# Block products of a triangular inverse issued in interleaved pairs, and the final norm's statistics taken for several row tiles at once

## The chip, the cores and the metric

The kernel runs on one core of one Trainium2 chip. The metric is the device time of one execution in microseconds; the time of a kernel is the median of three runs.

## The reference

One inference step of a one-layer decoder: 512 prompt rows and 8 sample rows of width 1024 go through a first norm, one combined input projection, two mixers side by side (sparse attention and a gated DeltaNet), an output projection, a squared-ReLU MLP and a final norm. Two places matter here.

In the DeltaNet, prompt rows are cut into chunks; for each chunk and head a unit lower triangular matrix is inverted:

```python
lmat = jnp.where(strict, jnp.einsum('...id,...jd->...ij', kb, k) * decay, 0.0)
tmat = lax.linalg.triangular_solve(eye + lmat, jnp.broadcast_to(eye, lmat.shape),
                                   left_side=True, lower=True, unit_diagonal=True)
```

At the very end every row is normed:

```python
y = xf * lax.rsqrt(jnp.mean(xf * xf, axis=-1, keepdims=True) + EPS)
return (y * g.astype(jnp.float32)).astype(x.dtype)
```

## The kernel before, in words

The kernel works on 4 chunks of 128 rows and 8 heads, so 32 matrices of 128x128, held in the tile LU (called M in this part, `M[row, m, column]`, m from 0 to 31).

**The weight stream.** All big products are units of one list (`units`): a unit takes a 128-column slice of a weight matrix (a load of 512 KB on SP's queue into one of 4 buffers, line 352), splits it in two parts on ACT and DVE (lines 398 to 402), and multiplies in 24 products per half of the rows (lines 450 to 453). Units called "a" (ada, line 257) make modulation vectors: two loads of 512 KB, then `quarters` (line 163), which issues products of 32 weight columns for four column groups of the array in turn, all 128 rows high, and two small products after it. Units may have a gate that opens only when other work was issued.

**Order.** `run` (line 475) merges generators with this stream: a `yield x` says that x * 1.6 us of stream products (by the program's own count, `pe_time`) may go ahead of the generator's next step. What the generators issue has a higher priority than the stream (line 484). The final order on each engine is set at build time by a list scheduler with a simulated timeline.

**The inverse** is in `triangular` (lines 1012 to 1122). The 32x32 blocks on the diagonal (called A, B, C, D, at partitions 0, 32, 64, 96) are inverted element by element on DVE; then off-diagonal blocks follow from products of 32x32 blocks (lines 1089 to 1105) and of 64x64 blocks (lines 1107 to 1122). `blocks` (line 1080) takes one PSUM bank, issues one product per matrix into it, 16 or 8 of one kind in a row, and returns it; DVE or ACT then take the bank out (lines 1092, 1093, 1100, 1101, 1104, 1110, 1119, 1121). Each of these fp32 products shows as two weight loads and two matmuls in the trace. Four kinds follow one another:

- first, 64 products of 32x32: rows B of the array into columns A, and rows D into columns C (lines 1090, 1091);
- second, 96 of 32x32: rows A into columns A, rows C into columns C, rows A into columns B (lines 1098, 1099, 1103);
- third, 32 of 64x64: upper half of the rows (64 to 127) into the lower half of the columns (line 1109);
- fourth, 32 of 64x64: lower half of the rows into the lower half of the columns (line 1115).

Banks with the tags "sc" and "pt" are four in all (line 142), given out in turn. After `triangular`, `recurrence` (line 1129) uses LU; the stream units left at that point are ada units, and then units whose gate `recurrence` opens. TA, iv and St are tiles of a pool of 5 buffers (`q4`).

**The end** is `final` (line 1920), called for row tiles 0 and 1, and then for 2, 3 and 4 (4 holds the sample rows). As the last projection's columns come in, a tile's 128x128 pieces are transposed on PE; after 4 pieces ACT squares and sums 512 columns (line 1936). Then, tile by tile: DVE adds two sums, `rstd` (line 273) scales on DVE and takes the power -1/2 on GpSimd (line 277), DVE and ACT scale the two halves (lines 1946, 1947), and SP stores both (line 1949).

## Time and profile before

| | us |
|---|---|
| three runs | 1317.97, 1320.69, 1319.63 (median 1319.63) |
| profiled execution | 1317.83 |
| its span, first to last instruction | 1315.8 |
| mean granted clock of TensorE in the span | 0.967 of full speed |
| PE busy in the span | 1230.0 (93%) |
| DVE, ACT, GpSimd busy | 845.6, 647.7, 237.9 |

A time in the trace counts from the first instruction of the span. PE is the matmul part of TensorE, PEld its weight loads, POOL is GpSimd, SP and ACT with a q are queues that issue transfers. An arrow "<-" before a name gives what ended an engine's idle time. A group's mean is the time of one instruction from start to end; matmuls overlap in the pipeline, so the distance of two starts, not the mean, is what one costs.

### The profile page before, as it was taken

The page shows a single profiled execution, that of the slowest core. Times are in us where ns is not written, and L with a number is a line of the kernel's source. Part 1 is how long each engine was busy: PE and PEld are TensorE (multiplying, and loading weights), DVE is VectorE, ACT ScalarE, POOL GpSimd, SP SyncE. Part 2 cuts the span into 40 slices and gives each one's busy share as a digit, 9 for nine tenths or more (in the row PEclk, how much of TensorE's full clock was granted, in tenths as well). Part 3 has the DMA queues.
Part 4 walks back from the last instruction along what each step waited for, and adds up shares of the span by engine and source line. Part 5 has one row for each costly group of instructions (what it writes and reads, how often), then busy time and mean ns, then how long its engine had stood idle before and what let it go on. Part 6 is the DMA issues. An engine that isn't in the chain of part 4 may idle for free.

```text
span 1315.8 us, 26700 instructions
## 1 busy us (share of the span) xinstructions
PE 1230.0 (93%) x10356; PEld 1161.2 (88%) x10356; DVE 845.6 (64%) x2294; ACT 647.7 (49%) x1552; POOL 237.9 (18%) x326
## 2 busy tenths in 40 slices
PE   4898899999989999899998899999999999999997
PEld 2698899989978989687788798989999999999997
DVE  2585868795356788886777787886843334334355
ACT  3484847754234345655555766673543133133134
POOL 2111110112121110321221332330331031030000
PEclk9899999999689999899999899999999999999999
DMA  8852412334252445335434221452723333333433
GB/s 255 231 163 75 134 36 65 99 84 130 73 148 68 129 118 153 113 108 164 136 98 153 74 71 49 128 161 66 208 65 97 89 91 95 97 91 87 133 108 114
DMA packets 235874, 149.82 MB, mean 114 GB/s; under 512 B 10330, under 2 KB 231058, under 8 KB 235484
## 3 DMA queue, kind: packets, MB, share of 16 engines
q1 hardware_dynamic: 226436, 135.84, 36.4%
q0 software_dynamic: 2240, 6.38, 1.8%
q10 hardware_dynamic: 7072, 5.90, 1.5%
q8 instruction: 81, 1.33, 0.4%
q14 instruction: 45, 0.37, 0.1%
HBM read 136.87 MB, written 15.60 MB: 116 GB/s over the span
## 4 chain that ended last, share of the span: by engine, by line
PE 45%; DVE 7%; ACT 3%; DMA 2%; issue 2%; POOL 1%; POOLq 0%; SPq 0%; ACTq 0%; DVEq 0%
PE bpg L153 36%; PE bsp L160 3%; PE bek L153 3%; PE bsp L153 2%; PE bek L169 1%; DVE wl L402 1%; DVE ptl L1490 1%; DMA raw<-in_w_in 1%; DMA raw<-in_w_up 1%; ACT ps L1458 0%; DMA raw<-in_w_out 0%; DVE wh L400 0%; ACT pw L1458 0%; DVE hl L1516 0%; DVE ps L1434 0%
## 5 line engine op out<-in xcount | busy, mean ns | idle before, releaser
L153 PE MATMUL bpg<-hh,wh 128*128 128x256 f32 (+1 forms) x1168 | 342.3, 293 | 5.9 <-ACT LU L705 1.9
L153 PE MATMUL bpg<-hh,wl 128*128 128x256 f32 (+1 forms) x1168 | 337.0, 289 | 1.8 <-DVE wl L402 1.8
L153 PE MATMUL bpg<-hl,wh 128*128 128x256 f32 (+1 forms) x1168 | 337.7, 289 | 0.0
L153 PEld LDWEIGHTS bpg<-hh,wh 128*128 128x128 f32 x1168 | 225.4, 193 | 11.6 <-ACT LU L705 2.5
L153 PEld LDWEIGHTS bpg<-hh,wl 128*128 128x128 f32 x1168 | 224.3, 192 | 4.2 <-DVE wl L402 3.1
L153 PEld LDWEIGHTS bpg<-hl,wh 128*128 128x128 f32 x1168 | 225.2, 193 | 1.8 <-issue 0.6
L402 DVE TENSOR_TENSOR wl<-raw,wh 128x1024 fp32r<-128x1024 f32 x149 | 182.4, 1225 | 66.9 <-PE bpg L153 35.8
L153 PE MATMUL bpg<-act,wh 128*128 128x264 f32 (+1 forms) x1024 | 186.7, 284 | 0.0
L398 ACT CAST wh<-raw 128x1024 fp32r<-128x1024 f32 x117 | 121.5, 1048 | 119.2 <-PE bpg L153 54.6
L153 PEld LDWEIGHTS bpg<-act,wh 128*128 128x128 f32 x1024 | 157.9, 188 | 0.1
L153 PE MATMUL bpg<-act,wl 128*128 128x264 f32 (+1 forms) x512 | 145.1, 284 | 0.2 <-DVE wl L402 0.2
L153 PE MATMUL bpg<-h2h,wl 128*128 128x256 f32 (+1 forms) x448 | 126.7, 283 | 0.3 <-DVE wl L402 0.3
L153 PE MATMUL bpg<-h2h,wh 128*128 128x256 f32 (+1 forms) x448 | 126.6, 283 | 0.0
L153 PE MATMUL bpg<-h2l,wh 128*128 128x256 f32 (+1 forms) x448 | 126.4, 282 | 0.0
L1842 POOL TENSOR_TENSOR r<-r 128x520 f32<-128x520 f32 (+2 forms) x40 | 60.1, 1502 | 285.7 <-ACT r L1841 281.4
L1805 DVE SCALAR_TENSOR_TENSOR o_dn<-bpg,consts,o_dn 128x256 f32<-128x256 f32 x80 | 38.2, 483 | 102.7 <-PE bpg L153 102.7
L153 PEld LDWEIGHTS bpg<-act,wl 128*128 128x128 f32 x512 | 96.3, 188 | 0.5 <-DVE wl L402 0.4
L1841 ACT ACTIVATE r<-bpg 128x256 f32<-128x256 f32 (+1 forms) x64 | 24.6, 386 | 137.1 <-PE bpg L153 137.1
L153 PEld LDWEIGHTS bpg<-h2h,wl 128*128 128x128 f32 x448 | 84.3, 188 | 0.5 <-DVE wl L402 0.5
L153 PEld LDWEIGHTS bpg<-h2l,wh 128*128 128x128 f32 x448 | 84.4, 188 | 0.0
L153 PEld LDWEIGHTS bpg<-h2h,wh 128*128 128x128 f32 x448 | 84.3, 188 | 0.0
L153 PE MATMUL bsp<-K,qst 128*128 128x256 f32 (+6 forms) x288 | 69.1, 319 | 5.8 <-DVE rounded L1481 2.0
(633 smaller groups left out, 2478.4 us busy)
## 6 DMA issues: line engine op xcount, KB each, us to landing
raw<-in_w_in SPq DMA_DIRECT2D x68, 512.0 KB
wa<-in_w_ada SPq DMA_DIRECT2D x48, 512.0 KB
raw<-in_w_down SPq DMA_DIRECT2D x40, 512.0 KB
raw<-in_w_up SPq DMA_DIRECT2D x36, 512.0 KB
raw<-in_w_out SPq DMA_DIRECT2D x12, 512.0 KB
Sx<-in_state_dn SPq DMA_DIRECT2D x16, 256.0 KB
out_s_dn<-Sx SPq DMA_DIRECT2D x16, 256.0 KB
pg<-in_cache_k_slc SPq DMA_DIRECT2D x16, 128.0 KB
```

The source lines that it names most:

```text
L153: nc.tensor.matmul(out, lhs, rhs, start=start, stop=stop)
L160: nc.tensor.transpose(out, in_, idn)
L169: r = nc.tensor.matmul(out[32 * j:32 * j + 32], lhs(j, s), rhs(j, s), start=start and s == 0, stop=stop and s == n - 1)
L398: nc.scalar.copy(out=wh, in_=raw)
L402: nc.vector.tensor_tensor(wl[:, 0:kp], raw[:, 0:kp], f32(wh[:, 0:kp]), op=ALU.subtract)
L1490: nc.vector.tensor_tensor(lo, pt, f32(hi), op=ALU.subtract)
L1805: nc.vector.scalar_tensor_tensor(xi[:, q], p[:, 0:n], mod[:, m + i, 0:1], xi[:, q], op0=ALU.mult, op1=ALU.add)
L1841: yield from halves(P, lambda c, p: nc.scalar.activation(r_[:, c], p, AF.Relu), hv)
L1842: nc.gpsimd.tensor_tensor(r, r, r, op=ALU.mult)
```

## The change

The products of the inverse are issued in an interleaved order, and land differently:

- first kind: the two sorts alternate product by product, into two banks as before;
- second kind: all three sorts alternate, into three banks at once (before: two after each other, and the third with a bank of its own later);
- third kind: even matrices go to the lower half of the columns and odd ones to the upper half, alternating, into one bank on all 128 partitions. X2, the copy of that result, is now one tile of 128 partitions, taken out in 2 copies of 128x512 (before: 4 of 64x512);
- fourth kind: even matrices use the lower half of rows and columns, odd ones the upper half of both, alternating, into one bank. The bank's two halves are taken out side by side by ACT and DVE.
- TA is one tile of 128 partitions, even matrices below and odd ones above; its fills are as many and as large as before, its results are written in 4 pieces of 32x256 (before: 2 of 32x512).

The yields in this part add up to 7 (before: 16).

In `final` the second half of the columns is squared in two pieces, 384 columns as soon as the seventh transpose is done and 128 after the eighth. The sums are added and the root is taken once for all tiles of the call (128x2 or 128x3). The store of the first half of the columns goes out from ACT's queue, that of the second half from SP's.

```diff
@@ -1069,56 +1069,61 @@ triangular
-        TA = [kb4(q4, (1024,), F32, "TA", "q4")[0:64].rearrange("p (m c) -> p m c", m=16) for _ in range(2)]
...
+        TA = kb4(q4, (1024,), F32, "TA", "q4").rearrange("p (m c) -> p m c", m=16)
+        for o in range(2):
+            nc.scalar.copy(out=TA[o * 64:o * 64 + 32, :, 0:32], in_=td[0:32, o:32:2])
+            nc.scalar.copy(out=TA[o * 64 + 32:o * 64 + 64, :, 32:64], in_=td[32:64, o:32:2])
...
-        def blocks(tag, q, lhs, rhs, ms, n):
-            p = bank(tag)[q].rearrange("p (m c) -> p m c", c=n)
+        def blocks(*parts, ms, n):
+            ps_ = [bank(tag)[q].rearrange("p (m c) -> p m c", c=n) for tag, q, _, _ in parts]
             for i, m in enumerate(ms):
-                mm(p[:, i], lhs(m), rhs(m), start=True, stop=True)
-            return p
+                for p, (_, _, lhs, rhs) in zip(ps_, parts):
+                    mm(p[:, i], lhs(m), rhs(m), start=True, stop=True)
+            return ps_
         for hf in range(2):
-            pa = blocks("sc", A_, lambda m: M[B_, m, A_], lambda m: M[B_, m, B_], hv[hf], 32)
-            pb = blocks("pt", C_, lambda m: M[D_, m, C_], lambda m: M[D_, m, D_], hv[hf], 32)
+            pa, pb = blocks(("sc", A_, lambda m: M[B_, m, A_], lambda m: M[B_, m, B_]),
+                            ("pt", C_, lambda m: M[D_, m, C_], lambda m: M[D_, m, D_]), ms=hv[hf], n=32)
...
-            yield 2
+            yield 1
...
-            pa = blocks("sc", A_, lambda m: td[A_, m], lambda m: tl[A_, m], hv[hf], 32)
-            pb = blocks("pt", C_, lambda m: td[C_, m], lambda m: tl[C_, m], hv[hf], 32)
+            pa, pb, pc_ = blocks(("sc", A_, lambda m: td[A_, m], lambda m: tl[A_, m]),
+                                 ("pt", C_, lambda m: td[C_, m], lambda m: tl[C_, m]),
+                                 ("sc", B_, lambda m: tl[A_, m], lambda m: td[A_, m]), ms=hv[hf], n=32)
...
-            yield 2
-            pa = blocks("sc", B_, lambda m: tl[A_, m], lambda m: td[A_, m], hv[hf], 32)
-            nc.vector.tensor_scalar(TA[hf][B_, :, A_], pa, -1.0, None, op0=ALU.mult)
+            for o in range(2):
+                nc.vector.tensor_scalar(TA[o * 64 + 32:o * 64 + 64, hf * 8:hf * 8 + 8, A_], pc_[:, o:16:2], -1.0, None, op0=ALU.mult)
             yield 1
...
+        def pairs(tag, lhs, rhs, n):
+            p = bank(tag).rearrange("p (m c) -> p m c", c=64)
+            for i in range(8):
+                for o, q in enumerate((H0, H1)):
+                    mm(p[q, i], lhs(n * 8 + i, o), rhs(n * 8 + i, o), start=True, stop=True)
+            return p
+        for n in range(2):
+            p = pairs("pt" if n else "sc", lambda i, o: M[H1, 2 * i + o, H0], lambda i, o: M[H1, 2 * i + o, H1], n)
+            (nc.scalar.copy if n else nc.vector.tensor_copy)(out=X2[:, n * 8:n * 8 + 8], in_=p)
             yield 0.5
         nc.gpsimd.memset(M[H1, :, H0], 0.0)
-        yield 2
+        yield 1
...
+        for n in range(2):
+            p = pairs("pt" if n else "sc", lambda i, o: TA[(H0, H1)[o], i], lambda i, o: X2[(H0, H1)[o], i], n)
+            nc.scalar.mul(M[H0, n * 16:n * 16 + 16:2, H1], p[H0], -1.0)
+            nc.vector.tensor_scalar(M[H0, n * 16 + 1:n * 16 + 16:2, H1], p[H1], -1.0, None, op0=ALU.mult)
             yield 0.5
@@ -1931,22 +1936,27 @@ final
+                c = {3: slice(0, 512), 6: slice(0, 384), 7: slice(384, 512)}.get(k)
+                if c is not None:
+                    e = t2("fsq")[0:n, c]
+                    nc.scalar.activation(e, p[:, c], AF.Square, accum_out=ss[0:n, j, max(k - 5, 0):max(k - 5, 0) + 1])
...
+        nt = len(ts)
+        r = ss[:, 0:nt, 0]
+        for i in (1, 2):
+            nc.vector.tensor_tensor(r, r, ss[:, 0:nt, i], op=ALU.add)
+        rstd(r, r, D)
         for j, t in enumerate(ts):
...
-            nc.vector.tensor_tensor(r, r, ss[0:n, j, 1:2], op=ALU.add)
-            rstd(r, r, D)
...
-                nc.sync.dma_start((yp_ap[:, t, :] if t < 4 else ys_ap)[:, hf * 512:(hf + 1) * 512], y[t, hf])
+                (nc.sync if hf else nc.scalar).dma_start((yp_ap[:, t, :] if t < 4 else ys_ap)[:, hf * 512:(hf + 1) * 512], y[t, hf])
```

## Rows read from the trace of the kernel before

**Rows 1.** Page, part 1: busy us, share of the span and instructions of each engine.

```profile
PE 1230.0 (93%) x10356; PEld 1161.2 (88%) x10356; DVE 845.6 (64%) x2294; ACT 647.7 (49%) x1552; POOL 237.9 (18%) x326
```

**Rows 2.** Windows: busy us of PE, PEld, DVE, ACT, POOL; granted clock, DMA share, GB/s.

```profile
330.00:334.00 4.00, 4.00 (x144) 4.00 (x141) 1.36 (x2) 1.09 (x3) 0.94 (x1) 1.00 0.92 280
334.00:338.00 4.00, 4.00 (x109) 4.00 (x106) 1.36 (x2) 1.02 (x2) 0.95 (x1) 0.67 0.16 54
...
350.00:356.00 6.00, 6.00 (x54) 5.88 (x54) 1.40 (x3) 1.07 (x2) 0.78 (x1) 0.50 0.00 0
356.00:360.00 4.00, 4.00 (x29) 2.63 (x30) 2.04 (x4) 1.65 (x5) 0.00 (x0) 0.59 0.23 68
```

**Rows 3.** Groups, 328 to 356 us: xcount, busy us, mean ns of one, idle before it.

```profile
L153 PE MATMUL bsp<-iv 32*32 32x32 f32 x192 | 8.3, 222 | 0.0
...
L153 PE MATMUL bsp<-LU 64*64 64x64 f32 x64 | 7.1, 312 | 0.0
L153 PE MATMUL bsp<-iv,TA 64*64 64x64 f32 x64 | 7.1, 312 | 0.0
...
L153 PE MATMUL bsp<-LU 32*32 32x32 f32 x128 | 4.1, 192 | 0.0
```

**Rows 4.** Timeline of PE, runs of one group merged: start us, length us.

```profile
329.95 3.71 PE L153 MATMUL bsp<-LU 32*32 32x32 f32 x121
...
341.77 6.45 PE L153 MATMUL bsp<-LU 64*64 64x64 f32 x58
...
355.24 0.69 PE L160 MATMUL bek<-consts,kvt 128*128 128x128 f32 x2
```

**Rows 5.** Timeline of PE where one run of products meets the next.

```profile
333.60 0.19 PE L153 MATMUL bsp<-iv 32*32 32x32 f32 x1
333.60 0.19 PE L153 MATMUL bsp<-LU 32*32 32x32 f32 x1
333.63 0.19 PE L153 MATMUL bsp<-iv 32*32 32x32 f32 x1
...
348.33 0.31 PE L153 MATMUL bsp<-LU 64*64 64x64 f32 x1
348.39 0.31 PE L153 MATMUL bsp<-iv,TA 64*64 64x64 f32 x1
348.43 0.31 PE L153 MATMUL bsp<-LU 64*64 64x64 f32 x1
```

**Rows 6.** Groups that take products out of PSUM: xcount, busy us, mean ns, idle before.

```profile
L1092 DVE COPY iv<-bsp 32x512 f32<-32x512 f32 x2 | 1.4, 678 | 3.0 <-PE bsp L153 3.0
L1101 ACT ACTIVATE LU<-bsp 32x512 f32<-32x512 f32 x2 | 1.2, 588 | 5.3 <-PE bsp L153 5.3
```

**Rows 7.** Timeline behind the block products; in brackets the idle time before and its end.

```profile
357.26 1.94 PE L169 MATMUL bek<-wa,consts 128*32 128x256 f32 x16
...
359.22 0.92 SPq L252 DMA_DIRECT2D wa<-in_w_ada  x2
...
366.17 1.94 PE L169 MATMUL bek<-wa,consts 128*32 128x256 f32 x16 [2.37 <-DMA wa<-in_w_ada]
```

**Rows 8.** End of the timeline, and groups (min/median/max ns) nearest to its new instructions.

```profile
1307.62 0.60 ACT L1936 ACTIVATE fsq<-bsp 128x512 f32<-128x512 f32 x1 [6.59 <-PE bsp L160]
...
1309.36 1.33 ACT L1947 ACTIVATE fo<-fo,consts 128x512 f32<-128x512 f32 x2
...
1311.53 0.74 DVE L1946 SCALAR_TENSOR_TENSOR fo<-bek,consts,fg 8x512 f32<-8x512 f32 x1 [0.65 <-POOL consts L277]
1312.28 0.86 SPq L1949 DMA_DIRECT2D out_y_sample<-fo  x2
...
L277 POOL TENSOR_TENSOR f__4363<-f__4363,consts x1: 1012/1012/1012, 388.8 to 388.8; 128x4 f32<-128x4 f32 x1
...
L592 ACT COPY nrm<-bek 128x128 f32<-128x128 f32 x4 | 1.1, 262 | 3.6 <-PE bek L169 3.6
...
L1771 ACTq DMA_DIRECT2D xt<-in_x_prompt x8: 334/334/439, 862.1 to 899.4; - x8
```

More of the change, by code (lines that the diff above doesn't have):

```diff
@@ L28 @@
 NKEEP = 8
-CW = 3736
+CW = 3752
 CR = 1024
@@ L1107, in triangular @@
-        for n in range(4):
-            ms = slice((n % 2) * 8, (n % 2) * 8 + 8)
-            p = blocks("pt" if n % 2 else "sc", H0, lambda m: M[H1, m, H0], lambda m: M[H1, m, H1], range(n * 8, n * 8 + 8), 64)
-            (nc.scalar.copy if n % 2 else nc.vector.tensor_copy)(out=X2[n // 2][:, ms], in_=p)
+        X2 = iv[1].rearrange("p (m c) -> p m c", m=16)
+        def pairs(tag, lhs, rhs, n):
[4 more added lines that the diff above has]
+            return p
@@ L1585, in hybrid_step @@
     sst = cst([128, 3, 3], F32)
-    sss = [cst([128, 3, 2], F32) for _ in range(2)]
+    sss = [cst([128, 3, 3], F32) for _ in range(2)]
     def nsa_sample():
```

22 lines of the change are left out of this document (4 added, 18 removed).

## The prediction

> **What bounds the kernel now.** I read the busy table first: PE is busy for 93% of the span [rows 1], so time is won where PE's own work becomes shorter or where PE waits. The windows around the changed part come next. From 330 to 356 us PE and its weight loads are busy all the time, DVE and ACT a quarter of it [rows 2], so in this stage PE is the bound, and the granted clock, full until 334, falls to 0.50 of it (from 2.4 to 1.2 GHz). The clock falls while PE is busy without a gap: what ran before the fall are products of 32x32, and the rows say no more of the cause. It is back at full only during the window from 356 on [rows 2].
>
> The groups of that stretch give the make-up: 128 + 192 matmuls of 32x32 and 64 + 64 of 64x64 [rows 3], two for each product of the inverse. The timeline gives the length: the main run begins at 329.95, and the first work behind it at 355.24 [rows 4], together 25.3 us. Distances of starts follow from the merged runs. 121 matmuls of 32x32 take 3.71 us, less 0.19 for the last one's own length: 0.029 us each, at full clock. 58 of 64x64 take 6.45 less 0.31 at half clock: 0.108 us each [rows 4].
>
> Then the junctions of two runs, which show what the change is after [rows 5]. Where the last products of the first kind (rows D into columns C) meet the first of the second kind (rows A into columns A), both sorts start at 333.60, and both again 0.03 later: each keeps its own step, and two run in the time of one. Where the third kind meets the fourth, starts alternate 0.05 and 0.06 apart, again two for one step of 0.108. The two differ there in rows alone. The ada products show column groups side by side: 16 matmuls of 256 columns take 1.94 us at half clock [rows 7]; at four times the step of a 64-column one they would take 16 x 0.43 = 6.9 us in sequence.
>
> **The change part by part.** All sums are against the profiled execution, 1317.83 us, which lies 1.8 us under the median of the runs shown; I add that back at the end.
>
> *Products.* Their number and shapes stay. By the junctions, each pair or triple costs one step. First kind: 128 matmuls are 64 steps of 0.029, 1.9 us. Second kind: 192 in triples are 64 steps; a mean clock of 0.67 from 334 to 338 [rows 2] puts the fall near 335.4, some 5.4 us after the start, so I take the first half at full clock, 0.9 us, and the second at half, 32 x 0.058 = 1.9 us. Third and fourth kind: 128 in pairs are 64 steps of 0.108, 6.9 us, at half clock as now. Sum: 11.6 us. Bounds: 25.3 if nothing overlaps; if the clock stays up, the second kind loses 0.9 and the last two halve to 3.5, which makes 7.3.
>
> *New waits for PSUM.* Before, each sort had a bank of its own and was taken out while the next one ran. Now three banks are filled at once, and there are four. The second kind's first triple needs the bank of the first kind's last half: its last matmul ends 0.2 us after its start, and DVE's copy takes 0.68 [rows 6], so PE stands for 0.9 us, with everything behind it in its queue. The second triple needs two banks of the first: again 0.2 + 0.68 = 0.9 (ACT's bank, 0.59, is earlier). The third kind needs the bank of the third sort, which DVE takes out after the first, in two half-size pieces of at most 0.68 each: at most 2.2 us after the triple's end, with 0.9 + 1.9 us between; no wait. Later banks come free a whole kind ahead. I take 1.8 us; bounds 0 (an ada product fills the gap) and 2.7 (the third kind waits too).
>
> *Take-outs.* X2's copies go from four to two, the last results' stay four, TA's go from two to four half-size pieces. They lie beside PE's pairs, except for the waits above; if that cover goes, each costs up to 0.68. The result, LU, is first used far behind the stage. TA's fills are as large as before: nothing.
>
> So the stage takes 11.6 + 1.8 = 13.4 us in place of 25.3: 11.9 us less.
>
> *Yields, 16 to 7.* That is 9 x 1.6 = 14.4 us less stream work issued ahead. What the stream has left here is ada units, of which three run behind the stage anyway (the first at 357.26, the last at 366.17), and then closed gates. I take nothing. What is late next are the weight loads: the queues are idle from 350 to 356 [rows 2], since all buffers are full; loads start again when the ada product at 357.26 is done (SP issues at 359.22), and the one at 366.17 still waits 2.37 us for its load [rows 7]. The release is PE's own work, which comes 11.9 us earlier, so loads and wait should move along. Bounds: 2.4 won if an ada product slips into a bank wait and starts the loads early; all 11.9 lost if the restart stays where it is.
>
> *The end.* PE sets the pace until the last transposes; the first square starts at 1307.62, and three squares of 0.6 follow one another [rows 8]. Now three of 128 columns: a copy of that size takes 0.26 [rows 8], so they end near 1308.6 with the last read of the sum. Two adds and a scaling on DVE, some 0.6. The power of 128x4 takes 1.01 [rows 8]; for 128x3 I take 0.9: 1310.1. Three scalings on DVE of 0.74 [rows 8] end at 1312.3; ACT has three of 0.67 (two take 1.33), each with a store's issue of 0.33 behind it on the same queue [rows 8] that holds the next: 1313.1. Before, the last scaling began at 1311.53 and the last issue ended at 1312.28 + 0.86 = 1313.1. I take 0; bounds: 0.8 won (a power of half the row's, issues beside the scalings), 0.6 lost (squares of 0.4 and the whole 1.01, with 0.1 more). In the first call the same work lies beside PE's stream: nothing.
>
> Sum: 1317.83 - 11.9 = 1305.9, and 1.8 for the median: **1307.7 us**.
>
> **A rule that speaks against it.** In the junctions the overlapping products of different rows wrote to different banks [rows 5]; in the fourth kind both members of a pair write to the same bank, on different partitions, from different rows. No row shows that case. The Trainium skill, page TensorEngine Tiling, section Restrictions and Gotchas, says that row tiles write to different PSUM banks and cannot access the same bank at the same time. By that rule the fourth kind alone would run in sequence, and its sum would be the one of the first rival below; the third kind has common rows and is not touched.
>
> **The rivals.**
>
> 1. *Pairs into one bank run one after the other.* The fourth kind then takes 64 x 0.108 = 6.9 us instead of 3.4: 1311.1 us. For it: no row shows such a pair overlapping. Against: ada's four column groups overlap on the same bank [rows 7], from common rows.
> 2. *More than forecast.* Denser products keep the clock at full (4.3 us more), or ada products fill the bank waits (up to 2.4 + 1.8): 1303.4 for either. Against the first: the clock fell within the 32x32 products, whose place now also has idle waits.
> 3. *The time comes back as a wait for weights.* With fewer yields the three ada products come behind the recurrence's first work, buffers stay full, and the loads restart about when they do now: 1318. For it: PE waits for a load at 366.17 already. Against: they are ready to run and the stretch behind the stage has gaps.
> 4. *Slower: no overlap in the pairs, while the waits are new.* The junctions show three products of each sort, with weights loaded ahead in long runs. PEld is busy throughout [rows 2]; if weight loads of two parts have to alternate, each product keeps its step, and the 1.8 to 2.7 us of bank waits stand on top: 1322.4. It decides if less than 1.8 of the 25.3 us overlaps. Against it: both junctions and the 16 ada products.
>
> **How the numbers follow.** The forecast 0.56, rival 1 0.16, rival 2 0.13, rival 3 0.08, rival 4 0.07. A difference under 0.2% (2.6 us) is about what a measurement of this kernel can't tell from no change. The forecast and rivals 1 and 2 are all faster by more: 0.85; rival 3 is no change: 0.08; rival 4 is slower: 0.07. The range: the forecast with its unknowns (waits 0 to 2.7, the end 0.8 won to 0.6 lost, loads up to 2.4) is 1302.7 to 1309.2; it must hold rivals 1 and 2 as well, with theirs: 1301.5 to 1313. That leaves out 0.15 and some edge.
>
> **What would show it.** Right: the stage's length near 13 us, starts of 64x64 matmuls 0.054 apart on average, two gaps of about 0.9 us on PE in the second kind, ended by DVE, the first ada product behind the stage some 12 us earlier, the last store's issue as long after the last transpose as now. Rival 1: the fourth kind at 0.108 per matmul with the third at 0.054. Rival 2: clock 1.00 through the stage. Rival 3: an idle time of PE near 10 us ended by a load. Rival 4: steps as now. The prediction is wrong if the stage shrinks as said and the span doesn't, or if the order behind it, which the build's scheduler sets anew, costs or saves over 5 us elsewhere.

## The result and the profile after

The changed kernel is slower: 1325.12 us (median of 7, 1323.37 to 1329.34) beside 1320.69 for the kernel before on the same chip, a ratio of 1.0057, 95% interval 1.003 to 1.0084. The forecast was 1307.7. The profiled execution took 1325.12, its span is 1322.5; the one of before had 1315.8. By the medians the loss is 4.4 us, by the two spans 6.7. The traces can only explain the spans, so 6.7 us are to be found, and 18.6 between the 11.9 that the forecast won and the 6.7 lost.

The busy table of the changed kernel, beside [rows 1]:

```profile
PE 1227.1 (93%) x10356; PEld 1156.7 (87%) x10356; DVE 842.1 (64%) x2291; ACT 648.4 (49%) x1561; POOL 241.3 (18%) x323
```

PE is busy 2.9 us less, so something did overlap, and it idles 9.6 us more (95.4 in place of 85.8). The windows of the stage, columns as in [rows 2]:

```profile
330.00:334.00 4.00, 4.00 (x154) 3.89 (x152) 1.22 (x3) 1.34 (x3) 0.37 (x1) 0.88 0.80 243
334.00:350.00 16.00, 15.16 (x227) 11.42 (x225) 4.04 (x9) 1.74 (x4) 1.52 (x2) 0.50 0.28 90
350.00:356.00 6.00, 6.00 (x103) 4.64 (x97) 0.29 (x2) 0.96 (x2) 1.80 (x1) 0.70 0.56 152
356.00:360.00 4.00, 1.00 (x24) 0.84 (x20) 3.11 (x4) 2.51 (x6) 0.00 (x0) 1.00 0.36 89
```

The clock's mean of 0.88 from 330 to 334 puts its fall to half (1.2 GHz) near 333.0, just where the second kind begins; before, it fell near 335.4, so the half of the second kind that the forecast took at full clock ran at half clock. PE had been busy without a gap ahead of both falls. New are also a clock that comes back to full within 350 to 356 (mean 0.70, where [rows 2] have 0.50), a PE that is busy for only 1.00 of the 4.00 us behind the products, and loads (0.56 of the DMA engines) from 350 to 356, where [rows 2] show none. What PE did, from its timeline (start us, length us; merged runs as in [rows 4]):

```profile
331.21 1.99 PE L153 MATMUL bsp<-LU 32*32 32x32 f32 x85
...
333.35 3.40 PE L153 MATMUL bsp<-iv 32*32 32x32 f32 x105
337.60 0.90 PE L153 MATMUL bsp<-iv 32*32 32x32 f32 x14 [0.84 <-issue]
...
341.29 0.47 PE L153 MATMUL bsp<-LU 64*64 64x64 f32 x2
341.69 0.32 PE L153 MATMUL bsp<-iv 32*32 32x32 f32 x4
341.94 0.48 PE L153 MATMUL bsp<-LU 64*64 64x64 f32 x4
342.35 0.31 PE L153 MATMUL bsp<-iv 32*32 32x32 f32 x2
342.58 0.47 PE L153 MATMUL bsp<-LU 64*64 64x64 f32 x2
...
348.13 0.52 PE L153 MATMUL bsp<-iv 32*32 32x32 f32 x10
...
351.40 1.65 PE L153 MATMUL bsp<-LU 64*64 64x64 f32 x26
...
360.57 1.93 PE L169 MATMUL bek<-wa,consts 128*32 128x256 f32 x16 [3.58 <-DVE LU L1126]
```

Read it in four places. (1) At 351.40, 26 matmuls of 64x64 (two for each product) take 1.65 us, less 0.31 for the last one's length: 0.054 each at half clock, half of the 0.108 that one took before, as the forecast had it for pairs. (2) From 341.29 to 348.58 the third kind runs *between* products of the second: 11 short runs of 64x64 and 11 of 32x32 (22 rows, six of them shown), 32 matmuls of each size, in 7.3 us. In pairs and triples at half clock they would be 16 x 0.108 + 32 x 0.019 = 2.3, so 5.0 are lost. Part of it is the change of size: from 341.94 to 342.58 one run of each size takes 0.64, two steps of 0.108 and two of 0.058 are 0.33 of that, and each of the two changes costs the rest, some 0.16. For 21 changes that is 3.3. The other 1.7 are lost pairing: a run of two 64x64 (341.29) takes as long to the next change, 0.40, as a run of four (341.94, 0.41). The order of the instructions is the build's: its scheduler takes what it finds ready, not what the program names next. (3) One wait at 337.60, for which the profile names no releaser ("issue"); the section on the stage comes back to it. (4) A wait of 3.58 us behind the products, ended by a take-out on DVE (L1126), which stood behind two weight splits (L402):

```profile
358.57 1.23 DVE L402 TENSOR_TENSOR wl<-raw,wh 128x1024 fp32r<-128x1024 f32 x1 [0.82 <-ACT wh L398]
359.82 0.69 DVE L1126 TENSOR_SCALAR LU<-bsp 64x512 f32<-64x512 f32 x1
```

The loads came earlier, and their splits now stand ahead of the take-out. How long PE then waits depends on its own pace: in e1, e9 and e17 below, whose order is the same up to here, the clock is at 0.50 from 345 to 360, the products end later, and this wait is 0.9 to 1.0, but the stage is no shorter.

Where the 6.7 us are: I cut both traces at the same five instructions (the 1537th matmul of the weight stream, L1181's first copy of w in the recurrence, which is L1186 after, the first of the attention masks, the 3073rd and the 3937th stream matmul) and took the windows between. The changed kernel:

```profile
0.00:320.03 320.03, 283.90 (x2303) 266.61 (x2304) 225.71 (x585) 191.10 (x429) 48.11 (x58) 0.96 0.46 128
320.03:373.10 53.07, 48.19 (x683) 39.50 (x682) 21.07 (x49) 14.30 (x32) 4.97 (x4) 0.77 0.46 140
373.10:508.09 134.99, 123.86 (x1062) 115.41 (x1060) 97.24 (x253) 57.17 (x124) 20.64 (x19) 0.96 0.35 98
508.09:804.90 296.81, 271.80 (x2207) 243.25 (x2206) 230.05 (x804) 179.92 (x542) 71.94 (x149) 0.97 0.38 112
804.90:967.39 162.49, 153.85 (x1239) 147.70 (x1238) 125.30 (x361) 95.05 (x251) 46.96 (x60) 0.97 0.45 121
967.39:1312.46 345.07, 344.50 (x2870) 343.78 (x2869) 139.41 (x232) 106.71 (x173) 47.86 (x32) 1.00 0.35 98
```

The kernel before, cut alike, has 321.12, 58.84, 129.46, 294.32, 157.51 and 345.06. So: 1.1 won ahead, **5.8 won in the stage** (11.9 forecast), **5.5 lost in the recurrence**, 2.5 lost in the middle, **5.0 lost late**, nothing in the MLP, and 0.5 in the end. The late row shows how: PE is busy 2.4 us more for nearly the same matmuls (1239, before 1243), as the clock is 0.97 in place of 1.00, and idle 2.6 more. The 2.5 of the middle are work that slid there: of the weight stream's matmuls it holds 985 (955 before), 4.9 us more of PE, and the recurrence 461 (488), 2.0 us less. So the recurrence lost its 5.5 although it has less to do.

Two places stand out in the lossy stretches, from the same timeline. In the recurrence:

```profile
452.31 2.15 DVE L1399 SCALAR_TENSOR_TENSOR Sx<-Sx,dsc,bsp 128x128 f32<-128x128 f32 x8
...
454.96 2.14 SPq L1342 DMA_DIRECT2D Sx<-in_state_dn  x2
...
455.50 0.27 PE L160 MATMUL bsp<-consts,vn 128*8 128x128 f32 x1
460.46 0.66 PE L169 MATMUL bsp<-Sx,dsc 128*32 128x128 f32 x8 [4.69 <-DMA Sx<-in_state_dn]
```

Head 1's state is updated, stored, and its buffer loaded with head 3's; PE is done with what stands ahead of head 3's read 0.8 us after the load's first issue and waits 4.69. In SP's queue a weight load that had been held for its buffer (issued 452.42) stands right ahead of these. And in attention:

```profile
826.66 1.48 DVE L402 TENSOR_TENSOR wl<-raw,wh 128x1024 fp32r<-128x1024 f32 x1
827.05 1.77 POOL L1476 TENSOR_SCALAR consts<-consts,scl 128x32 f32<-128x32 f32 x1
828.79 1.82 POOL L1476 TENSOR_SCALAR ps<-ps,scl 128x384 f32<-128x384 f32 x1
828.87 0.29 PE L160 MATMUL bsp<-consts 128*32 128x128 f32 x1 [1.10 <-POOL consts L1476]
829.03 1.20 DVE L402 TENSOR_TENSOR wl<-raw,wh 128x1024 fp32r<-128x1024 f32 x1
830.66 0.33 PE L160 MATMUL bsp<-consts,ps 128*128 128x128 f32 x1 [1.51 <-POOL ps L1476]
```

Two scalings on POOL take 1.77 and 1.82 us beside DVE's splits, and PE waits 1.10 and 1.51 for them; in the kernel before the same two take 0.73 and 0.58, as DVE was waiting for a weight load just then. Behind them the clock is low:

```profile
820.00:830.00 10.00, 7.73 (x73) 5.46 (x71) 9.88 (x37) 7.01 (x27) 4.77 (x5) 1.00 0.99 258
830.00:835.00 5.00, 4.33 (x24) 4.34 (x25) 1.49 (x6) 0.22 (x1) 3.55 (x8) 0.66 0.64 174
```

### The profile page after: what moved, and what is told of

Read it like the earlier page. It is cut to its first block, busy times and chain, and to the rows that moved or that the text cites. A ratio compares the mean times of both kernels' runs of the same rounds, so it can differ in the third digit from the quotient of the medians.

```text
span 1322.5 us, 26699 instructions
## 1 busy us (share of the span) xinstructions
PE 1227.1 (93%) x10356; PEld 1156.7 (87%) x10356; DVE 842.1 (64%) x2291; ACT 648.4 (49%) x1561; POOL 241.3 (18%) x323
## 4 chain that ended last, share of the span: by engine, by line
PE 78%; DVE 9%; ACT 5%; DMA 4%; issue 2%; POOL 1%; SPq 0%; POOLq 0%; DVEq 0%; ACTq 0%
PE bpg L153 55%; PE bsp L153 10%; PE bsp L160 5%; PE bek L153 3%; PE bek L169 3%; DVE wl L402 1%; DMA wa<-in_w_ada 1%; DVE X L899 1%; DMA xall<-in_x_prompt 1%; DMA raw<-in_w_in 1%; ACT wh L398 1%; PE bek L160 1%; DMA w1r<-in_cmp_w_v 1%; POOL r L1847 1%; DVE cy L572 1%
## 5 line engine op out<-in xcount | busy, mean ns | idle before, releaser
L402 DVE TENSOR_TENSOR wl<-raw,wh 128x1024 fp32r<-128x1024 f32 x149 | 183.3, 1232 | 62.9 <-PE bpg L153 34.7
L153 PEld LDWEIGHTS bpg<-act,wh 128*128 128x128 f32 x1024 | 157.7, 188 | 0.1
L153 PE MATMUL bpg<-h2h,wh 128*128 128x256 f32 (+1 forms) x448 | 126.6, 283 | 0.0
```

Source lines behind the costliest of these rows:

```text
L153: nc.tensor.matmul(out, lhs, rhs, start=start, stop=stop)
L402: nc.vector.tensor_tensor(wl[:, 0:kp], raw[:, 0:kp], f32(wh[:, 0:kp]), op=ALU.subtract)
```

## The experiments

Three theories. **Stage**: the pairs overlap, but the scheduler undoes the alternation and mixes the sizes. **Filling**: with the stage shorter and fewer yields, stream work no longer lies where later steps need cover. **Order**: an edit can make the build lay out anew the whole order behind it, and that alone moves the time by several us. The table has every kernel, cut at the same five instructions (us; the MLP and the end, which hardly move, are left out; ratio to runs of the kernel before on the same chip, with its interval).

| kernel | ahead | stage | recurrence | middle | late | span | ratio |
|---|---|---|---|---|---|---|---|
| before | 321.1 | 58.8 | 129.5 | 294.3 | 157.5 | 1315.8 | 1 |
| changed | 320.0 | 53.1 | 135.0 | 296.8 | 162.5 | 1322.5 | 1.0057 [1.003, 1.0084] |
| e1 blocks alone | 318.4 | 53.5 | 133.8 | 298.7 | 163.5 | 1322.3 | 1.0032 [1.0009, 1.0055] |
| e2 final alone | 317.0 | 58.9 | 129.3 | 294.9 | 160.5 | 1315.6 | 0.9993 [0.9974, 1.0012] |
| e3 old yields | 319.1 | 49.7 | 132.8 | 295.6 | 158.6 | 1310.9 | 0.9943 [0.9922, 0.9963] |
| e4 pinned | 319.7 | 48.6 | 130.7 | 293.2 | 156.8 | 1304.0 | 0.9906 [0.9881, 0.9931] |
| e5 32x32 first | 317.3 | 45.9 | 133.8 | 299.1 | 163.1 | 1314.2 | 0.9969 [0.9952, 0.9987] |
| e6 state on POOL | 321.2 | 53.8 | 132.8 | 300.4 | 160.7 | 1323.8 | 1.0071 [1.0053, 1.0088] |
| e7 before, pinned | 319.7 | 57.3 | 139.0 | 297.1 | 157.2 | 1324.9 | 1.0062 [1.0043, 1.0081] |
| e8 pinned, old yields | 318.6 | 52.8 | 134.9 | 298.9 | 159.6 | 1320.0 | 1.0001 [0.9979, 1.0023] |
| e9 four DMAs moved | 318.7 | 53.5 | 131.7 | 300.2 | 162.2 | 1321.9 | 1.0036 [1.0016, 1.0056] |
| e10 scalings on ACT | 319.3 | 52.4 | 133.6 | 298.7 | 155.9 | 1315.0 | 1.0005 [0.9987, 1.0022] |
| e11 e9 and e10 | 319.8 | 53.7 | 131.4 | 300.7 | 156.2 | 1317.3 | 0.999 [0.9973, 1.0007] |
| e12 e5, e9, e10 | 317.9 | 46.2 | 132.4 | 300.3 | 155.5 | 1307.8 | 0.9945 [0.9926, 0.9963] |
| e13 read later | 320.5 | 53.0 | 126.0 | 296.3 | 160.3 | 1311.0 | 0.995 [0.993, 0.997] |
| e14 e5, e10, e13 | 320.6 | 48.2 | 126.6 | 294.5 | 157.7 | 1302.4 | 0.987 [0.9838, 0.9902] |
| e15 before, e10, e13 | 320.1 | 60.0 | 122.8 | 295.8 | 156.8 | 1309.7 | 0.9955 [0.9933, 0.9978] |
| e16 before, e10 | 316.3 | 60.0 | 130.1 | 293.1 | 160.5 | 1314.6 | 1.0003 [0.9983, 1.0023] |
| e17 changed, e10, e13 | 322.4 | 56.7 | 126.1 | 294.8 | 160.2 | 1314.9 | 0.9947 [0.9926, 0.9968] |
| e18 e4, e10, e13 | 317.8 | 49.1 | 129.9 | 298.6 | 158.7 | 1309.3 | 0.9924 [0.9893, 0.9955] |

How much is one trace worth? Up to the recurrence the changed kernel, e1, e9, e10, e11, e13 and e17 have PE's matmuls in one and the same order, and so have, but for a few, before, e2, e15 and e16. The first seven show 318.4 to 322.4 us ahead and 52.4 to 56.7 in the stage (mean clock 0.67 to 0.77), the other four 316.3 to 321.1 and 58.8 to 60.0. So one order moves by some 4 us from execution to execution, and a difference of that size between two single traces is not yet an edit's. The 1.1 ahead is nothing; the stage's gain stands, 5.7 us by the means. The recurrence stands too: 133.6 to 135.0 with the changed kernel's order (e1, e10), 129.3 to 130.1 with that of before (e2, e16). Stage, recurrence and middle together hold the same stream work in every kernel, whatever slides between them: their sum is 484.7 to 486.0 in the changed kernel, e1 and e10, and 482.6 to 483.2 in before, e2 and e16. What the stage won was more than given back in the two stretches behind it.

### Which part (e1, e2)

e1 is the kernel before with the block products of the change, e2 the one with the rest of it:

```diff
-        def blocks(tag, q, lhs, rhs, ms, n):
+        def blocks(*parts, ms, n):
...
```

```diff
-    sss = [cst([128, 3, 2], F32) for _ in range(2)]
+    sss = [cst([128, 3, 3], F32) for _ in range(2)]
...
```

> The kernel before with the block products of the triangular inverse changed and the final norm left as it was. If the loss comes from the block part (its stage, or what its fewer yields do to the stream behind it), this gives the changed kernel's time, 1324 to 1327 us. If the loss needs the final part or the larger table of constants, it comes out under 1318. If the loss is only that the build lays the whole order out anew with every edit, the time is neither: anything from 1308 to 1328, with the block stage as long as in the changed kernel and the difference in the stretches behind it.

> The kernel before with the final norm's part alone (squares in three pieces, one power for the call, stores from two queues, constants 16 wider). By the end's own sum nothing changes: 1320 to 1321.5 us. If the order of the whole program is drawn anew by any edit and that is worth several us, the time can stand 3 to 8 us off in either direction while the stage of the triangular inverse keeps its 25 us.

e1 1323.17 us, e2 1318.54. The loss is the block part's: e1 has the changed kernel's order on PE up to 1286 us, so it is as good as a second measurement of it (1.0032 beside 1.0057), and its stretches have the same pattern. The final part is worth nothing that can be measured. Its stretches move by up to 4 us, one against the other.

### The stage (e3, e4, e5, e7, e8)

e3 raises the yields:

```diff
             nc.scalar.copy(out=tl[C_, hs[hf]], in_=pb)
-            yield 1
+            yield 2
...
-            yield 1
+            yield 3
         X2 = iv[1].rearrange("p (m c) -> p m c", m=16)
...
-            yield 0.5
+            yield 1
...
-        yield 1
+        yield 2
```

> The changed kernel with the yields of the block products raised to the sum of the kernel before (16 in place of 7), so that some 14 us more of stream work is issued among the block products. If the loss is that the stream's units slide from this stage into later generators, the recurrence behind starts where it did before and the time falls under 1316. If the stage itself is what costs (each switch between 32x32 and 64x64 products and the lost alternation), the time stays at 1323 to 1327 or gets worse, as ada's products are mixed in as well.

1312.15 us. The stage shrinks to 49.7: with 3 us of yields between them, the third kind no longer mixes with the second. This run can't tell yields from mixing. e4 holds the products in the program's order:

```diff
+        def pin(out, lhs, rhs):
+            with tc.high_priority(20000) if made else nullcontext():
+                r = nc.tensor.matmul(out, lhs, rhs, start=True, stop=True)
+            if made:
+                tc.keep_in_program_order(r)
+            made.append(r)
+            pe_time[0] += rhs.shape[-1] * 4 / 2400.0
...
-                    mm(p[:, i], lhs(m), rhs(m), start=True, stop=True)
+                    pin(p[:, i], lhs(m), rhs(m))
```

> The changed kernel with the block matmuls held in the order of the program: pairs and triples really alternate, and no product of 64x64 runs between those of 32x32. If the stage lost its gain by sorts that ran one after the other and by the some 6.9 us in which the second and the third kind alternate, the stage shrinks by 4 to 7 us and the time falls to 1316 to 1320. If what is won in the stage is handed back later whatever its length (loads, recurrence, filling), the stage shrinks and the time stays within 2 us of the changed kernel, 1323 to 1327. If the order behind is drawn anew and that decides, the time is off by another amount, with the difference in the stretches behind 370 us.

1306.95 us, 11 faster than before, more than either theory gave it. Its stage, from PE's timeline:

```profile
330.56 1.58 PE L1087 MATMUL bsp<-LU 32*32 32x32 f32 x88
...
333.79 1.14 PE L1087 MATMUL bsp<-iv 32*32 32x32 f32 x90
337.11 0.32 PE L1087 MATMUL bsp<-iv 32*32 32x32 f32 x4 [2.18 <-issue]
...
340.18 1.92 PE L1087 MATMUL bsp<-iv 32*32 32x32 f32 x94
342.03 1.97 PE L1087 MATMUL bsp<-LU 64*64 64x64 f32 x32
...
346.92 1.97 PE L1087 MATMUL bsp<-LU 64*64 64x64 f32 x32 [1.05 <-ACT LU L1116]
348.99 1.97 PE L1087 MATMUL bsp<-iv,TA 64*64 64x64 f32 x32
```

Matmuls of 32x32 in pairs come at (1.58 - 0.19) / 87 = 0.016 us each, in triples at (1.14 - 0.19) / 89 = 0.0107, and 64x64 in pairs at (1.97 - 0.31) / 31 = 0.0535 at half clock. Third and fourth kind take the same 1.97 for 32: the fourth kind, whose pairs write one bank from different rows, overlaps as well. By these steps all products together are about 11.6 us (11.6 forecast). The waits are 2.18 and 1.05, 3.2 (1.8 forecast), but neither is a wait for a bank of PSUM:

```profile
334.97 0.68 DVE L1115 TENSOR_SCALAR LU<-bsp 32x512 f32<-32x512 f32 x1 [0.90 <-PE bsp L1087]
337.41 0.85 DVE L1118 TENSOR_SCALAR TA<-bsp 32x256 f32<-32x256 f32 x2 [1.76 <-PE bsp L1087]
...
345.21 1.04 ACT L398 CAST wh<-raw 128x1024 fp32r<-128x1024 f32 x1 [5.44 <-DMA raw<-in_w_in]
346.27 0.59 ACT L1116 ACTIVATE LU<-bsp 32x512 f32<-32x512 f32 x1
```

The first one, up to 337.11, falls between matmuls of one triple, whose banks it already has: DVE's take-out of that triple's first sort is over at 335.65, and DVE then itself waits for PE (337.41). What the trace does show is a packet on queue 8, which brings PE its instructions, 16 KB at a time; some 256 matmuls and weight loads start between two packets. It starts in the window 334.4 to 334.5 here, and in 335.0 to 335.1 in the changed kernel:

```profile
q8 instruction: 1, 0.02, 67.2%
...
q8 instruction: 1, 0.02, 66.0%
```

The fifteen kernels of the table with the changed products have 16 such waits between 32x32 matmuls, 0.3 to 2.9 us long, and every one ends 2.2 to 2.7 us after the start of such a packet. The five with the products as before have none. So PE seems to stand for its own instructions, which pairs and triples use up faster; no run tried to change that. The second wait is the take-out L1116 on ACT, which stood behind the cast of a weight (345.21) and the 5.44 us that ACT had waited for its load: the same as the 3.58 in the changed kernel.

e7 holds the kernel before's own products in order, with the same helper:

```diff
-                mm(p[:, i], lhs(m), rhs(m), start=True, stop=True)
+                pin(p[:, i], lhs(m), rhs(m))
```

> The kernel before with its own block matmuls held in the order of the program, sort by sort, as the pairs were held in the pinned kernel. If the pinned kernel's gain comes from pairs that overlap, this gains nothing: its stage stays at 23 to 27 us, and the time is 1316 to 1321 (or a little more, since the few overlaps at the junctions go). If the holding itself brings the gain, as a better draw of the order behind, it falls to 1306 to 1312.

1326.05 us. Its stage on PE:

```profile
332.19 8.33 PE L1084 MATMUL bsp<-iv 32*32 32x32 f32 x191
340.45 6.76 PE L1084 MATMUL bsp<-LU 64*64 64x64 f32 x61
...
347.28 6.71 PE L1084 MATMUL bsp<-iv,TA 64*64 64x64 f32 x61
```

Held alike, the stage of the changed kernel takes 48.6 and that of before 57.3, 8.7 us more, although it holds only 56 matmuls of the stream in place of 103 (7.8 us of PE in place of 15.7): the overlap is worth more than the difference. Holding gains nothing by itself; the 9.5 us that e7 loses in the recurrence (4.1 of them a wait for the state, and 12 stream matmuls more) were expected by nobody. I put them down to the order, which no run tests.

e5 lets the 32x32 products go first, so that no 64x64 one comes between; the order behind the stage stays nearly the changed kernel's:

```diff
-                    mm(p[:, i], lhs(m), rhs(m), start=True, stop=True)
+                    with tc.high_priority(20000): mm(p[:, i], lhs(m), rhs(m), start=True, stop=True)
```

> The changed kernel with the 32x32 block products put ahead of everything else that is ready on PE, so that no 64x64 product runs between them; what stands behind the stage keeps almost the order of the changed kernel (246 lines of PE's order differ, all of them near the stage). If the some 6.9 us in which 32x32 and 64x64 products alternate are a cost of their own, they shrink to about 2.5 (36 products of 32x32 in triples at 0.019 and 34 of 64x64 in pairs at 0.054 each), and the time falls by 4 to 5 us, to 1319 to 1321. If the loss sits in the order behind the stage, as the unchanged order behind it would repeat, at least the late wait for the state's load (4.7 us) and the later loss of some 6 us stay, and the time does not fall below the kernel before. If only those count, it stays at 1323 to 1327.

1313.99 us; against the changed kernel 8 us by the two spans, 11 by the two ratios (1.0057 and 0.9969). That is about twice the 4 to 5 expected, and it went below the kernel before, which the second theory had excluded. The stage has 45.9 us in place of 53.1. On PE:

```profile
334.85 2.00 PE L153 MATMUL bsp<-iv 32*32 32x32 f32 x78 [0.73 <-issue]
336.78 1.97 PE L153 MATMUL bsp<-LU 64*64 64x64 f32 x32
```

The 7.3 us of mixing are gone, and so is the wait of 3.58 behind the products. The state's wait (4.0 us) and the late collision are there as in the changed kernel, recurrence and late stretch are as long. So three losses stand side by side. The same edit is all that parts e12 from e11 and e14 from e17 below: the stage falls from 53.7 to 46.2 and from 56.7 to 48.2, the ratio from 0.999 to 0.9945 and from 0.9947 to 0.987. The mixing is thus shown three times, at 7 to 9 us of the stage.

> The pinned kernel with the yields raised to the sum of the kernel before (16 in place of 7). If the fewer yields cost something behind the stage, this is 2 to 5 us under the pinned kernel: 1302 to 1305. If the yields are worth nothing in themselves, and the kernel with the old yields was faster only because a yield of 3 kept the 64x64 products from mixing with the 32x32 ones, it is within 2.5 us of the pinned kernel, 1304 to 1309.5. If more ada units in the stage only push the recurrence back, it is slower by up to 6 us, 1309 to 1313.

e8 (e4 with e3's yields): 1319.22 us, 12 more than e4, outside all three expectations. Its stage has 52.8 us with 7.1 idle, its recurrence the wait for the state (4.5). More yields gain nothing once the order is held, which speaks for the mixing as e3's gain, without showing it; of the 12 that they cost here the stage has 4.2, and the rest is not explained.

### The recurrence (e6, e9, e13)

> The changed kernel with the loads and stores of the sample state (Sx) issued from POOL's queue and no longer from SP's, where in the changed kernel two weight loads stand ahead of them, the second held until its buffer is free (7.7 us behind the first), and PE then waits 4.7 us for the state. If that queue is the cause of this wait, the wait goes to under 2 us and the recurrence keeps 4 to 5 us more of what the stage won: 1319 to 1321. The order of the rest is drawn anew by this edit as well; a time outside 1316 to 1324 with the wait gone would say that this redrawing is worth more than the wait. If the state's own store and its buffer are late, the wait stays at 4 to 5 us.

```diff
-                nc.sync.dma_start(Sx[h][hf], sd[:, hf * 4:hf * 4 + 4, h])
+                nc.gpsimd.dma_start(Sx[h][hf], sd[:, hf * 4:hf * 4 + 4, h])
...
-                nc.sync.dma_start(sdo[:, hf * 4:hf * 4 + 4, h], Sx[h][hf])
+                nc.gpsimd.dma_start(sdo[:, hf * 4:hf * 4 + 4, h], Sx[h][hf])
```

e6: 1327.23 us. The wait falls to 1.6 us, but PE now waits 9.4 in three waits for POOL's scalings (4.6 in four in the changed kernel), and the order is another. It doesn't tell. e9 moves four DMAs only:

```diff
-                nc.sync.dma_start(Sx[h][hf], sd[:, hf * 4:hf * 4 + 4, h])
+                (nc.gpsimd if h == 3 else nc.sync).dma_start(Sx[h][hf], sd[:, hf * 4:hf * 4 + 4, h])
...
-                nc.sync.dma_start(sdo[:, hf * 4:hf * 4 + 4, h], Sx[h][hf])
+                (nc.gpsimd if h == 1 else nc.sync).dma_start(sdo[:, hf * 4:hf * 4 + 4, h], Sx[h][hf])
```

> The changed kernel with four DMAs alone moved from SP's queue to POOL's: the two stores of head 1's state and the two loads of head 3's, which in the changed kernel stand in SP's queue behind a weight load that waits for its buffer, and for which PE then waits 4.7 us; of PE's order 764 lines of some 7400 differ. If that queue causes the wait, it goes, and with it the low clock that follows: the recurrence shrinks from 135.0 us to 129 to 131, and the time falls by 3 to 6 us, to 1319 to 1322. If the wait only moves to another load or to the stream, the recurrence keeps its 133 to 136 us and the time its 1323 to 1327.

1322.17 us, and on its timeline:

```profile
454.68 1.49 POOL L1342 DMA_DIRECT2D Sx<-in_state_dn  x2
...
459.30 0.65 PE L169 MATMUL bsp<-Sx,dsc 128*32 128x128 f32 x8 [4.35 <-DMA Sx<-in_state_dn]
```

The queue was not the cause: this part of the theory falls. The chain from the start of the update over store and load to the read takes some 8 us in either queue (452.31 to 460.46 in the changed kernel, 451.48 to 459.30 here), and the read stands too close behind it. In the kernel before, 7 stream matmuls lie in between, and PE waits 2.05 for DVE there instead. e13 puts the read later:

```diff
         for h in range(8):
-            yield 4
+            yield 9 if h == 2 else 4
...
-            yield 4
+            yield 0.5 if h == 2 else 4
```

> The changed kernel with the read of head 3's state put later by one pause of its generator (9 in place of 4 us of PE time ahead of it, 0.5 in place of 4 behind it); the order ahead of 450 us stays as it is, the one behind is drawn anew. If PE waits 4.7 us because the read stands too close behind the load, this wait goes to under 1 us and the recurrence shrinks from 135.0 to 129 to 132 us. By how much the time falls depends on the order behind as well: 1318 to 1323 if that repeats the late loss, 1312 to 1317 if it doesn't. If PE simply has nothing to do there, the idle time comes back within the recurrence, which keeps 133 to 136 us.

1312.83 us. The wait for the state is gone, and the recurrence has 126.0 us, 9.0 less, twice the wait.

### The late stretch (e10, e16) and the sums

e10 puts six scalings on ACT:

```diff
-                nc.gpsimd.tensor_scalar(x, x, sc[:, a_ * 3 + b_:a_ * 3 + b_ + 1], 1.0, op0=ALU.mult, op1=ALU.mult)
+                nc.scalar.mul(x, x, sc[:, a_ * 3 + b_:a_ * 3 + b_ + 1]) if (g, i, pr) == (3, 2, 0) else nc.gpsimd.tensor_scalar(x, x, sc[:, a_ * 3 + b_:a_ * 3 + b_ + 1], 1.0, op0=ALU.mult, op1=ALU.mult)
```

> The changed kernel with the six scalings of one attention step (near 827 us) on ACT in place of POOL. In the changed kernel two of them take 1.77 and 1.82 us on POOL beside DVE's weight splits (0.72 and 0.58 for the same in the kernel before, where DVE was waiting for a load at that time), PE waits 1.1 and 1.5 us for them, and the granted clock is at 0.66 behind it. If that is what the late stretch loses, it shrinks by 3 to 4.5 us of its 162.5 (2.6 of wait and up to 1.7 of clock): 1320 to 1322.5. If it is only one of several such places, each made good later, the late stretch stays at 161 to 164 us and the time at 1323 to 1327. The work is the same in both.

1317.93 us, and the late stretch has 155.9 us, 6.6 less, more than expected. The same windows as above:

```profile
820.00:830.00 10.00, 8.91 (x87) 7.02 (x86) 9.71 (x36) 8.79 (x31) 0.38 (x2) 1.00 1.00 251
830.00:835.00 5.00, 5.00 (x45) 5.00 (x44) 3.05 (x11) 2.58 (x8) 2.06 (x5) 1.00 0.48 126
```

The clock stays at full, here and in the whole late stretch; two later dips of the changed kernel (0.67 in 880 to 884, 0.77 in 932 to 936) are gone too. e1, e5 and e9 have the collision as well, with the same 1.77 and 1.82, and late stretches of 162.2 to 163.5; e11 and e12, with e10's edit, have 156.2 and 155.5.

> The kernel before with the six scalings near 827 us on ACT alone. In the kernel before none of the six is slowed (0.58 to 0.73 us each) and PE does not wait for them, so by the theory of the collision nothing is won: the late stretch stays at 156 to 158.5 us and the time at 1317 to 1321. If ACT is simply the better engine for them, the stretch shrinks by 2 us or more and the time falls under 1316.

e16 (the kernel before with e10's edit): 1318.74 us, no gain, as expected of a kernel without the collision; its late stretch of 160.5 is longer than expected, made up elsewhere (ahead, where the edit does nothing).

> The changed kernel with both of these edits (four state DMAs on POOL's queue, six scalings on ACT) and the block products as in the changed kernel. If the two losses are separate and add up, the time falls by 6 to 10 us, to 1315 to 1319, about the kernel before or a little under. If they are draws of the order that come back elsewhere when one is taken away, it stays at 1321 to 1327.

> All three: the 32x32 block products ahead of all else on PE, so that no 64x64 product runs between them, four state DMAs on POOL's queue, and six scalings on ACT. If stage, recurrence and late stretch are the three places of the loss, the sum is that of the kernel with the block products ahead (1314, with its own wait of 4.0 us for the state and the same late collision) less 6 to 10 us: 1304 to 1309, where the forecast was. If the losses behind the stage come back elsewhere, it stays at 1311 to 1316.

e11 (e9 and e10) 1318.26: what was expected of a sum, but it is e10's part alone, since e9's edit leaves the wait (4.4 us). e12 (with e5) 1311.69, inside its second expectation for the same reason (4.5 us of wait); 0.45% of it are e5's.

> The changed kernel with the 32x32 block products ahead of all else, the read of head 3's state later, and the six scalings near 827 us on ACT. If the stage (45.9 us up to the first step of the recurrence in place of 53.1), the wait for the state and the late collision are the three places of the loss, the three together give the forecast or better: 1303 to 1308. If one of them comes back elsewhere, it is 1309 to 1314.

e14 (e5, e10, e13): **1303.01 us**, the fastest of all, 0.987 of the kernel before, and the time of the forecast. How much of that is the change's own only the next runs tell.

> The kernel before with the same two edits behind the stage (the read of head 3's state later, six scalings on ACT). It has neither the wait for the state nor the collision at 827 us, so by the theory of three places it gains nothing: 1316 to 1321. If the two edits are better orders in themselves, it gains as the changed kernel does and falls to 1309 to 1314; what they bring there was then not the change's loss.

e15 (the kernel before with e10 and e13): 1311.73, so the theory of three places failed here. The later read shortens a recurrence without the wait too, by 6.7 us, but 34 stream matmuls (3.4 us of PE) have slid from it into the middle. Over stage, recurrence and middle together, which hold the same work, the edit takes before from 483 to 478.6 and the changed kernel from 485 to 475.3. So some 5 of its 10 us, about the wait for the state, were the changed kernel's own loss, as far as single traces tell; the rest is a better order for either.

> The changed kernel, block products as they are, with the read of head 3's state later and six scalings on ACT. The kernel before with the same two edits stands at 0.9955 of the kernel before. If the change is worth what its stage gains (53.1 us up to the recurrence in place of 58.8, 5.7 less, with the switches still in), this is at 0.990 to 0.993, 1305 to 1309 us. If the change gives its gain back behind the stage whatever the order there, it is at 0.9945 to 1.000, 1311 to 1318.

> The pinned kernel (block products really in pairs and triples) with the same two edits. If the stage's gain (10.7 us) and the later read's gain in the recurrence (6.7 us in the kernel before) add up, this is at 0.983 to 0.988, 1296 to 1303 us. If the pinned kernel's time was a good draw of the order behind, it loses that draw here and stands at 0.989 to 0.996, 1304 to 1313.

e17 (changed, with e10 and e13) 1312.25, e18 (e4 with the same) 1308.6. Both missed the first expectation. As compiled, the change is worth nothing beside e15 (0.9947 and 0.9955). e17 also gains nothing on e13 (0.995): in e13's order no scaling on POOL is slowed, so the late collision belongs to one order and is not a fixed part of the loss. With the mixing removed as well the change is worth 0.85% beside e15 (e14, 0.987), 11 us, or 8.7 by the two medians; the stages differ by 11.8 (48.2 and 60.0), where 11.9 was forecast. And e4's time was perhaps a good draw of the order: two edits that helped others gain nothing on it (0.9924 beside 0.9906, the intervals overlap), and its middle stretch is 5.4 us longer.

## Why the prediction was wrong, point by point

**"By the junctions, each pair or triple costs one step."** The mechanism was right and its price too: about 11.6 us in e4, 11.6 forecast. The step that failed is the unspoken one behind it, that PE would issue the products in the order of the program. In the changed kernel part of each kind runs unpaired (85 matmuls of the first at 0.021 each, pairs take 0.016; 105 of the second at 0.030 at half clock, triples would take 0.019), and the third kind comes between products of the second: 7.3 us for what pairs and triples take 2.3. The stage won 5.8 instead of 11.9; with the order mended it won 11.8 (e14 beside e15). The Trainium skill, page TensorEngine Tiling, section Tiling Modes, says that a change of the tiling mode drains the engine; the trace agrees that a change costs time, some 0.16 us for each of 21 at half clock. The junctions that I read had no change of size in them [rows 5]. The clock, which the sum kept at full for half of the second kind, fell ahead of it; that is 0.9 us.

**"New waits for PSUM", 1.8 us.** No wait for a bank was seen. PE stood 0.84 us in the second kind in the changed kernel and 2.18 in e4, but for its instructions, as far as the traces tell; and the third kind, where I had said "no wait", waits 1.05 in e4 for a take-out behind a weight's cast. That such waits are near the forecast size is luck.

**"Yields, 16 to 7 ... I take nothing", and "loads and wait should move along".** This failed. The weight loads did come earlier, and that started two collisions: DVE's splits ahead of a take-out for which PE waited 3.58 us, and, 470 us later, splits beside POOL's scalings. e10 shows the second one's price, 6.6 us of the late stretch, more than the 5.0 lost there. The read of the state lost its cover of stream work, 4.7 us of wait, of which e13 and e15 leave some 5 to the change itself. The middle stretch's 2.5 are stream work that no longer lay in the recurrence.

**"The end ... I take 0."** 0.5 lost, within its bounds; the last stores are late by the power on POOL (0.86 us for 128x3, 0.9 forecast) and the squares' last reads.

**Rival 1, one bank.** Refuted: the fourth kind's 32 take 1.97 us like the third's. The Trainium skill, TensorEngine Tiling, Restrictions and Gotchas, forbids row tiles the same bank; here pairs of tiles on different rows and columns wrote one bank, on different partitions, at the rate of the third kind, and the measurement decides. **Rival 2**, a clock at full, did not come: it fell earlier than before. **Rival 3**: no idle time near 10 us ended by a load came, but its thought, that the time comes back behind the stage, is what happened. **Rival 4** had the sign by the wrong cause: the steps did halve. The last sentence, that the order behind could cost over 5 us elsewhere, named the outcome and was given no chance and no place in the range. One order differs by some 4 us in a stretch from execution to execution, and another order moved a recurrence by 9.5 (e7); that was the size of the doubt.

## What to carry to other kernels

When a build's scheduler orders the instructions, an overlap that needs two sorts to alternate is only won if the order is held, and runs of different tile sizes must be kept apart; read the order of the instructions off the timeline before believing the sum. What a shorter stage sets free (loads, splits, casts) starts earlier and meets other work, so its price is paid far behind: cut both traces at the same instructions, compare stretch by stretch, and count what work lies in each, since stream work slides across the cuts and one trace is good to a few us only. An edit's worth is the difference between two kernels with the same surroundings, and here the block products cost 0.3 to 0.6% as built (e1 and the changed kernel), nothing beside e15, and won 0.85% once the sizes were kept apart (e14 against e15). The 1.6% between e4 and e7, both held in order, has e7's bad recurrence in it.

## What the runs showed of the hardware

Two products of 64x64 on different rows and columns of the array overlap fully when they write to the same bank on different partitions (0.0535 us a matmul at half clock, as with common rows). A change between 32x32 and 64x64 matmuls costs some 0.16 us at half clock. With 32x32 matmuls in pairs and triples PE stood 0.3 to 2.9 us, and each of 16 such waits ended 2.2 to 2.7 us after the start of a 16 KB packet of PE's instructions. A scaling on POOL that takes 0.58 us took 1.82 beside a subtraction of 1024 columns on DVE, and one of 32 columns took 1.77, beside such a subtraction and a cast, in place of 0.29 to 0.73. The Trainium skill, page SBUF — State Buffer, section SBUF: two separate sides, has a port pair that DVE and GpSimd hold one at a time for a whole instruction, whichever starts first. The trace agrees for the first of the two, which ended at 828.82, when DVE's subtraction and the cast behind it had ended; the second started 0.24 us ahead of DVE's subtraction by the trace, whose spans on POOL are rough, and yet ended behind it. The granted clock fell towards half (1.2 GHz) late in the changed kernel three times: to 0.66 from 830 to 835, behind 7.73 us busy of 10.00; to 0.67 from 880 to 884, behind 1.65 of 4.00; to 0.77 from 932 to 936, behind 5.95 of 8.00. In e10 PE is busy 8.91, 3.79 and 8.00 in the same windows, and the clock is 1.00 in all six.
